# One order of products for a whole decoder trunk, with its moving averages moved to another stage

## The chip, the core and the metric

The kernel runs on one core of a Trainium2 chip. The metric is the time of one execution on the device in microseconds (us), smaller is better. Engines are named as the profile names them: PE (TensorE, the matrix engine; PEld are its weight loads), DVE (VectorE), ACT (ScalarE), POOL (GpSimd) and SP (SyncE, which only issues DMAs here).

## The reference, cut

One layer, 2048 rows of width 1024, all in 32-bit floats:

```python
mod = silu(c) @ w_ada + b_ada;  shift, scale, gate = split(mod, 3)
u = x * (1 + scale) + shift
q, k, v, a_gate, p_in, p_gate, m_a, m_p = split(u @ w_in, ...)
a = sliding_window_sink_attention(q, k, v) * silu(a_gate)      # 16 heads, window 128
a = a @ w_attn_proj
p = grouped_linear(causal_moving_average(p_in) - p_in)         # windows 2, 4, 8, 16 by group
p = (p * pool_scale) * silu(p_gate);  p = p @ w_pool_proj
y = (sigmoid(m_a) * a + sigmoid(m_p) * p) @ w_out * (1 + gate)
x = layer_norm(2 ** 0.25 * x + y)
```

The grouped linear map is folded into the pooling weights ahead of the moving average (`wmix_d`), so the average is taken of a product's result (`px_d`).

## The kernel before

**Products.** Every large matrix product is cut into blocks (`Quad`, "block" below): two weight tiles against one chunk of 1024 rows, as a 2x2 by 2x2 block product that needs seven multiplications in place of eight. A block's seven products are B11, T1 (stage F), T2, B21 (stage S), T3, B22 (stage Th) and T4 (stage L). A product is 12 matmuls of 128x512: 32-bit weights are split into a high and a low part (`w_set`: ACT casts the high part, DVE or POOL subtracts it for the low part) and three partial products are summed, four times over the depth. The seven right-hand sides are the sums of one chunk's input, held in SBUF as `set_B..`, `set_T..`. For its weight sums a block needs POOL: `sum1` (1 addition, after the load of `W` and `A22`), `mid` (2) before the split of S, `late` (1) before the split of Th. At most four `w_set` tiles live at once.

**Stages.** There are 74 blocks, 518 products. The stages are named after their tile pools: `g0` (modulation of x, keys, values; two groups of two blocks), `o0` (13 single blocks, with the attention of the first chunk laid between their matmuls: the "overlay"), `e0` (four groups of two blocks, mostly gates), the same for the second chunk (`g1`, `o1`, `e1`), then `mix`: four phases of two groups (projections) and the output phase of four groups with the layer norm. Between phases all seven sets are exchanged (`turn_sets`: each half is loaded by SP, cast by ACT, subtracted by DVE).

**What sets the order.** In `o0` and `o1` the order on each engine is the order of writing (`Ordered`, by `solos`): a block's splits stand two products ahead of their use, the first split of the next block one to two. In all stages of pairs (`ring`, `front`, `back`) a split is written directly ahead of its product, through plain `nc.scalar`, `nc.vector`, and a scheduler of the framework sets the order on ACT and DVE; `W` is loaded behind the T3 product of a block two blocks earlier. Work around the products hangs on product counts (`hooks`, `defer`). SP's queue is always in written order.

**The overlay.** After each third of a product (`beat`) a credit grows; when it reaches one, one attention step is written into PE's stream (scores, transposes, values; `lg<-kk,qs`, `pt<-ident,L`, `pv<-pth,vv`), with its softmax on DVE and ACT. Here also stand the moving averages (`window_jobs`): 32 jobs in each overlay, each of 256 columns. A job loads `vb` from `px_d`, adds 1 to 4 shifted copies on POOL (`nxt`), subtracts on DVE and stores `pw_d`. They start 25 products into the overlay. `pool_job`, in `e0` and `e1`, loads `pw_d` and the gate, multiplies, forms sums and stores them for `mix`.

```python
def window():                               # window_jobs, POOL, 256 columns
    cur, k = job["v"], 1
    while k < w:
        nx = ph.t.tile([P, 16 + C2], F32, tag="nxt", bufs=2, name="nxt")
        pool.tensor_tensor(nx[:, lo_t:], cur[:, lo_t:], cur[:, lo_t - k : 16 + C2 - k], ALU.add)
```

**Other places.** The sums of the second chunk's input (`sums_to(ph, u1_d, ...)`) are made in `e0`. The gate row of the modulation is summed in `g0` (8 loads of 512 KB, 8 reductions on DVE) and turned around through DRAM on ACT's DMA queue at the start of `g1` (`gate_rows`). In `back`, the second block of the first group of a stage begins with one extra matmul into its bank (`ph.fresh`) directly ahead of ACT's copy and of T2.

Of the kernel before, what the change touches and what calls it, by code (L numbers as in the profile page):

```python
# [19 lines left out]
P = 128  # L20
D = 1024
# [38 lines left out]
def kernel(  # L60
# [40 lines left out]
    carry = cp.tile([P, 3, 16], F32, name="carry")  # L101
# [51 lines left out]
    on = {"act": nc.scalar, "dve": nc.vector}  # L153

    def pin(flag):
        on.update({"act": act, "dve": dve} if flag else {"act": nc.scalar, "dve": nc.vector})

    class Pools:
# [33 lines left out]

        def own(self, name="x", dt=F32, tag="x"):
            return self.t.tile([P, CH], dt, tag=tag, bufs=self.bufs[tag], name=name)

        def c(self, name="c", dt=F32):
            self.n += 1
            if "more" in self.bufs and self.n % (4 + self.bufs["more"]) >= 4:
                return self.own(name, dt, "more")
            return wp.tile([P, CH], dt, tag="c", bufs=4, name=name)  # L200
# [42 lines left out]

    class Quad:
        def __init__(self, srcs, consume):
            self.srcs, self.consume = srcs, consume

        def load_w(self, ph, q=nc.sync, a12=True):
# [7 lines left out]
        def load_last(self, ph, own, q=nc.sync):  # L256
            self.a22 = ph.last(own)
            q.dma_start(self.a22, self.srcs[1][:, CH:])

        def load(self, ph, own, q=nc.sync, a12=True):  # L260
            self.w, self.a22 = ph.weights(), ph.last(own)
            x = self.w
            q.dma_start(x[:, 2, :], self.srcs[1][:, 0:CH])
            q.dma_start(self.a22, self.srcs[1][:, CH:])
            if a12:
                q.dma_start(x[:, 0::3, :], by_two(self.srcs[0]))
            else:
                q.dma_start(x[:, 0, :], self.srcs[0][:, 0:CH])

        def sum1(self, e=nc.gpsimd):  # L270
            e.tensor_tensor(self.w[:, 1, :], self.w[:, 2, :], self.a22, ALU.add)  # L271

        def mid(self, e=nc.gpsimd):
# [4 lines left out]
        def late(self, e=nc.gpsimd):  # L278
# [18 lines left out]
    def pair_split(ph, raw, a=nc.scalar, d=nc.vector):  # L297
        hi, lo = ph.split(), ph.split()
        a.copy(by_two(hi), raw)  # L299
        low(d, by_two(lo), raw, by_two(hi))  # L300
        return halves(hi, lo)

    def half_split(ph, raw, a=nc.scalar, d=nc.vector):
        s = ph.split()
        hi, lo = s[:, 0:CH], s[:, CH:]
        a.copy(hi, raw)
        low(d, lo, raw, hi)
        return hi, lo
# [19 lines left out]
    def front(ph, q, tick, beat=None):  # L328
        w = pair_split(ph, q.first())
        q.mid()  # L330
        a, b = bank(), bank()
        product(a, w[0], "B11", True, beat=beat)
        tick()
        product(b, w[1], "T1", True, beat=beat)
        tick()
        return a, b, None, None

    def back(ph, grp, opened, nxt, own, tick):
        st = []
        for x, (q, (a, b, c, w, *copy)) in enumerate(zip(grp, opened)):  # L340
            p5 = ph.p("p5")
            if w is None:
                c = bank("c1" if x else "lg")
                if x and ph.fresh:
                    t = sets["B11"][:, 0, 0, :]
                    mm(c, t[:, 0:P], t, start=True, stop=True, skip_group_check=True)
                    ph.fresh = False
                nc.scalar.copy(c, a)  # L348
                nc.scalar.copy(p5, b)
                w = pair_split(ph, q.second())[::-1]  # L350
                q.late()
                product(c, w[1], "T2")
            else:
                nc.vector.tensor_tensor(c, c, copy[0], ALU.add)
                nc.scalar.copy(p5, b)
            tick()
            nc.vector.tensor_tensor(b, c, p5, ALU.add)
            if not copy:
                product(a, w[0], "B21")
            tick()  # L360
            q.consume(ph, 0, 0, a)
            st.append((q, b, c, p5))
        w = {}

        def ask(q):
            defer(1, lambda: q.load(ph, own))
            defer(3, q.sum1)

        def third(x):
            w[x] = pair_split(ph, st[x][0].third())[::-1]  # L370
            if x < len(nxt):
                ask(nxt[x])

        def with_t3(x):
            q, b, c, p5 = st[x]
            product(c, w[x][1], "T3")
            tick()
            nc.vector.tensor_tensor(p5, c, p5, ALU.add)
            q.consume(ph, 1, 1, p5)

        def with_b22(x):
            q, b, c, p5 = st[x]
            product(b, w[x][0], "B22")
            tick()
            q.consume(ph, 0, 1, b)

        for x in range(len(st)):
            third(x)
            with_t3(x)
            with_b22(x)  # L390
        for q, b, c, p5 in st:
            w = half_split(ph, q.a22)
            product(c, w, "T4")
            tick()
            q.consume(ph, 1, 0, c)

    now, due = [0], []

    def defer(ticks, f):
        due.append((now[0] + ticks, len(due), f))  # L400

    def run_due(every=False):
        while due and (every or any(d[0] <= now[0] for d in due)):
            d = min(due, key=lambda d: d[:2])
            due.remove(d)
            d[2]()

    def ring(ph, groups, opened, hooks, nxt, after):

        pos = [0, 0]  # L410

        def tick():
            for f in hooks.get((pos[0], pos[1]), ()):
                f()
            for f in hooks.get((pos[0] - len(groups), pos[1]), ()):
                f()
            pos[1] += 1
            now[0] += 1
            run_due()

        for gi, grp in enumerate(groups):
            pos[:] = [gi, 0]
            own = gi % 2 == 0 and gi + 1 < len(groups)
            back(ph, grp, opened, (groups + [nxt])[gi + 1], own, tick)
            if gi + 1 < len(groups):
                opened = [front(ph, q, tick) for q in groups[gi + 1]]
        if after:
            return [front(ph, q, tick) for q in nxt]
        return None

    def solos(ph, quads, nxt, beat, hooks):

        seq = quads + nxt

        at = [0]

        def tick():
            for f in hooks.get(at[0], ()):
                f()
            at[0] += 1  # L440
            now[0] += 1
            run_due()

        w = pair_split(ph, seq[0].first())
        seq[0].mid()
        for i, q in enumerate(quads):
            hi, lo = ph.split(), ph.split()
            act.copy(by_two(hi), q.second())
            low(dve, by_two(lo), q.second(), by_two(hi))
            q.late(pool)  # L450
            ws = halves(hi, lo)[::-1]
            a, b = bank(), bank()
            product(a, w[0], "B11", True, beat=beat)
            c = bank()
            act.copy(c, a)
            tick()
            product(b, w[1], "T1", True, beat=beat)
            p5 = ph.p("p5")
            act.copy(p5, b)
            tick()  # L460
            hi, lo = ph.split(), ph.split()
            act.copy(by_two(hi), q.third())
            low(pool, by_two(lo), q.third(), by_two(hi))
            wt = halves(hi, lo)[::-1]
            product(c, ws[1], "T2", beat=beat)
            dve.tensor_tensor(b, c, p5, ALU.add)
            tick()
            product(a, ws[0], "B21", beat=beat)
            q.consume(ph, 0, 0, a)
            tick()  # L470
            wl = half_split(ph, q.a22, act, dve)
            product(c, wt[1], "T3", beat=beat)
            dve.tensor_tensor(p5, c, p5, ALU.add)
            q.consume(ph, 1, 1, p5)
            if i + 2 < len(seq):
                z = seq[i + 2]
                defer(1, lambda z=z: z.load_w(ph, sp))
                defer(2, lambda z=z: z.load_last(ph, False, sp))
                defer(5, lambda z=z: z.sum1(pool))
            tick()  # L480
            more = i + 1 < len(quads)
            if more:
                hi, lo = ph.split(), ph.split()
                act.copy(by_two(hi), seq[i + 1].first())
# [964 lines left out]
```

## Time and profile before

| | before |
|---|---|
| three runs | 1907.67, 1910.65, 1914.93 us (median 1910.65) |
| the profiled execution | 1913.9 us, of which its instructions span 1912.1 us |
| PE busy in it | 1723.5 us (90%), granted clock 0.959 on average |
| DVE, ACT, POOL busy | 1308.2, 932.5, 854.1 us |
| DMA | 382.19 MB, 200 GB/s |

The stages in the span: head 0 to 66.2 (eight products), rest of `g0` to 169.7, `o0` with four products of `e0` to 588.8, `e0` with four products of `g1` to 759.8, `g1` to 839.9, `o1` with four of `e1` to 1267.9, `e1` with four of `mix` to 1428.8, `mix` without and then with its output phase to 1737.8 and 1912.1. A row of a timeline gives start, length, engine, line, operation and in brackets the idle time before it and what ended it. In rows of helper functions the line is L56 (`Ordered`), so tiles name the work.

### The profile page before, as it was taken

Reading aid. Unit: us, or ns where it says so; the run is one execution under the profiler, and the core shown is the slowest. Engines: PE = TensorE matmul, PEld = TensorE weight load, DVE = VectorE, ACT = ScalarE, POOL = GpSimd, SP = SyncE. Lnnn points to the kernel's source line nnn. Section 1 sums busy time; section 2 is a strip of 40 time slices with the busy share of each in tenths; the row PEclk is TensorE's granted clock in tenths of the full one; section 3 lists DMA queues with packets and bytes.
Section 4 is the critical chain, followed back from the end, with each engine's and each line's share of the span. In section 5 each row is a group of like instructions: output and inputs, shape, how many; then the busy total and the mean of one; then the engine's idle time right before and its main releaser. Section 6 shows DMA issues by size and latency. Waiting matters only on the chain.

```text
span 1912.1 us, 25151 instructions
## 1 busy us (share of the span) xinstructions
PE 1723.5 (90%) x8061; PEld 1419.6 (74%) x8061; DVE 1308.2 (68%) x2221; ACT 932.5 (49%) x1764; POOL 854.1 (45%) x818
## 2 busy tenths in 40 slices
PE   6789999888888998799998888879999999998996
PEld 6578887676676777678887766768877777787885
DVE  5754778577663658558796776635675967769777
ACT  3444776556553335337775555523353442534452
POOL 3123354545555443453455456632232564356442
PEclk9899999999898999899999999889999999999998
DMA  8587455655346789694457544435895685767432
GB/s 320 171 266 232 133 165 181 184 155 156 118 140 221 258 304 334 222 291 158 146 175 209 165 147 133 128 105 163 292 357 165 222 274 176 242 218 264 172 133 99
DMA packets 237796, 382.19 MB, mean 200 GB/s; under 512 B 31184, under 2 KB 89312, under 8 KB 237664
## 3 DMA queue, kind: packets, MB, share of 16 engines
q1 hardware_dynamic: 233120, 371.87, 59.1%
q10 hardware_dynamic: 3232, 4.49, 0.8%
q0 software_dynamic: 1312, 4.22, 0.6%
q8 instruction: 64, 1.05, 0.2%
q14 instruction: 68, 0.56, 0.1%
HBM read 244.15 MB, written 139.49 MB: 201 GB/s over the span
## 4 chain that ended last, share of the span: by engine, by line
PE 52%; DMA 15%; DVE 13%; issue 6%; ACT 6%; POOL 5%; SPq 3%; POOLq 0%; DVEq 0%; ACTq 0%
PE mm L56 33%; PE lg L56 9%; PE c L56 7%; DMA pw_d<-nxt 3%; SPq L56 3%; PE pv L56 2%; PE pt L56 2%; DVE w_set L56 2%; DVE w_set L136 2%; ACT L L56 1%; DVE nxt L56 1%; POOL st L56 1%; DVE L L56 1%; POOL nxt L56 1%; DVE st L56 1%
## 5 line engine op out<-in xcount | busy, mean ns | idle before, releaser
L56 PE MATMUL mm<-set_B,w_set 128*128 128x512 f32 x2664 | 679.5, 401 | 48.7 <-ACT w_set L299 27.3
L56 PEld LDWEIGHTS mm<-set_B,w_set 128*128 128x128 f32 x2664 | 507.0, 193 | 166.0 <-ACT w_set L299 29.2
L56 PE MATMUL mm<-set_T,w_set 128*128 128x512 f32 x1824 | 475.6, 406 | 44.7 <-POOL w_set L56 24.4
L56 PEld LDWEIGHTS mm<-set_T,w_set 128*128 128x128 f32 x1824 | 349.4, 196 | 129.0 <-POOL w_set L56 28.3
L136 DVE TENSOR_TENSOR w_set<-W,w_set 128x1024 fp32r<-128x1024 f32 x142 | 199.5, 1407 | 155.5 <-ACT w_set L299 152.3
L299 ACT CAST w_set<-W 128x1024 fp32r<-128x1024 f32 x142 | 148.8, 1049 | 304.5 <-PE mm L56 234.9
L56 PE MATMUL c<-set_T,w_set 128*128 128x512 f32 x864 | 213.6, 396 | 22.9 <-ACT c L348 17.5
L56 PE MATMUL lg<-set_T,w_set 128*128 128x512 f32 x864 | 213.5, 395 | 4.8 <-DVE w_set L136 2.7
L56 PEld LDWEIGHTS c<-set_T,w_set 128*128 128x128 f32 x864 | 163.5, 190 | 62.0 <-ACT c L348 19.7
L56 PEld LDWEIGHTS lg<-set_T,w_set 128*128 128x128 f32 x864 | 163.3, 190 | 42.4 <-DVE w_set L136 3.5
L271 POOL TENSOR_TENSOR W<-W,A 128x512 f32<-128x512 f32 x46 | 68.6, 1492 | 269.4 <-DMA A<-in_win_dram 79.7
L56 POOL TENSOR_TENSOR W<-W 128x512 f32<-128x512 f32 x74 | 96.7, 1320 | 149.3 <-DVE w_set L56 78.1
L56 ACT ACTIVATE L<-L,nm 128x257 f32<-128x257 f32 (+1 forms) x256 | 126.8, 498 | 47.0 <-DVE nm L56 33.3
L56 ACT ACTIVATE L<-L,sm 128x256 f32<-128x256 f32 (+1 forms) x128 | 64.3, 503 | 150.8 <-DVE sm L56 150.3
L56 DVE CUSTOM_DVE_ANT_0 L<-lg,bt,nsink 128x256 f32<-128x256 f32 (+1 forms) x256 | 110.9, 469 | 38.8 <-PE lg L56 27.9
L280 POOL TENSOR_TENSOR W<-W 128x512 f32<-128x512 f32 x46 | 73.1, 1588 | 121.0 <-DVE w_set L136 113.4
L275 POOL TENSOR_TENSOR W<-W 128x512 f32<-128x512 f32 x48 | 77.5, 1615 | 107.5 <-DVE w_set L136 96.5
L56 PEld LDWEIGHTS lg<-kk,qs 128*128 128x128 f32 x512 | 80.1, 198 | 56.7 <-DVE nm L56 31.0
L56 PE MATMUL lg<-kk,qs 128*128 128x256 f32 (+1 forms) x512 | 87.4, 295 | 37.0 <-DVE nm L56 22.8
L56 DVE TENSOR_SCALAR L<-L,sm 128x256 f32<-128x256 f32 (+1 forms) x128 | 111.1, 868 | 4.5
L56 DVE TENSOR_TENSOR ptl<-pt,pth 128x512 fp32r<-128x512 f32 (+1 forms) x128 | 85.8, 670 | 31.3 <-ACT pth L56 31.0
L56 POOL TENSOR_TENSOR nxt<-nxt 128x256 f32<-128x256 f32 (+3 forms) x96 | 62.3, 649 | 82.3 <-DMA pw_d<-nxt 69.2
(216 smaller groups left out, 2583.6 us busy)
## 6 DMA issues: line engine op xcount, KB each, us to landing
W<-in_win_dram SPq DMA_DIRECT2D x40, 512.0 KB, 6.1
qs<-q_d SPq DMA_DIRECT2D x128, 128.0 KB, 3.9
W<-in_win_dram SPq DMA_DIRECT2D x46, 256.0 KB, 4.8
A<-in_win_dram SPq DMA_DIRECT2D x42, 256.0 KB, 5.0
ag_d<-sig SPq DMA_DIRECT2D x32, 256.0 KB, 3.4
q_d<-q_hi SPq DMA_DIRECT2D x32, 256.0 KB, 3.5
q_d<-q_lo SPq DMA_DIRECT2D x32, 256.0 KB, 3.9
mp_d<-sig SPq DMA_DIRECT2D x32, 256.0 KB, 6.2
```

Of the source, the lines that this page charges most:

```text
L56: return lambda *args, **kw: self.tc.keep_in_program_order(op(*args, **kw))
L136: engine.tensor_tensor(dst, src, as32(hi), ALU.subtract)
L271: e.tensor_tensor(self.w[:, 1, :], self.w[:, 2, :], self.a22, ALU.add)
L275: e.tensor_tensor(x[:, 1, :], x[:, 1, :], x[:, 0, :], ALU.subtract)
L280: e.tensor_tensor(x[:, 3, :], x[:, 3, :], x[:, 1, :], ALU.subtract)
L299: a.copy(by_two(hi), raw)
```

## The change

All phases go through one plan. `plan` lists the 518 products of all stages in order, `run` writes them out one by one on ordered queues. Each stage of a block is split two products ahead of its first product (later only where a `w_set` tile is not free); loads are tied to the block two ahead, also across phases. `ring`, `front`, `back` and `solos` go away.

- `window_jobs` and the tensor `pw_d` go away. `pool_job` now loads 512 columns of `px_d`, adds on POOL, subtracts on DVE, multiplies by the gate: 16 jobs in each of `e0` and `e1`, one every three products.
- The pooling gates pg0 and pg2 move ahead (to `g` and to the overlay), two blocks of merge gates move from there to `e`.
- The second chunk's input sums move from `e0` into `o0`, as eight `sums_job` of 256 columns.
- The gate row's sums move from `g0` to `e0`; its turn through DRAM goes from ACT's queue to SP's, the store in `e0`, the load in `g1`.
- Attention steps start after 12 beats (10 before) and come every 4.7 beats (5.2 before). Four products of the following stage no longer carry beats.
- `ph.fresh`'s extra matmul stands two stages earlier, with the copies of `c` and `p5` directly behind B11 and T1; gates of `mix` are loaded three products ahead; key tiles get room of their own.

```diff
+        for q, kind, p, k in stages:
+            mine = [slots[(n + j) % 4] for j in range(1 if kind == "L" else 2)]
+            hi = max(p - 2, mine[0] + 1, prev, 0)
+            lo = max(hi, mine[-1] + 1)
...
+        for q, z in zip(order, order[2:]):
+            p = q.at["Th"] + 1
+            loads.setdefault(p, []).append((z, "w"))
+            wait = not z.own and not q.own and not q.pair
+            limit = split_at[z] - 1
+            loads.setdefault(min(p + 1 if wait else p, limit - 1), []).append((z, "last"))
+            loads.setdefault(min(p + 4 if wait else p + 2, limit), []).append((z, "sum"))
...
-        start = [[kv_quad(s), ag[0]], [q[0], mp[0]]]
-        alone = [q[2], ag[2], x[0], x[2], q[4], ag[4], x[4], q[6], ag[6], x[6], ma[0], ma[2], ma[4]]
-        end = [[pg[0], pg[2]], [pg[4], pg[6]], [ma[6], mp[2]], [mp[4], mp[6]]]
+        start = [[kv_quad(s), ag[0]], [q[0], pg[0]]]
+        alone = [q[2], ag[2], x[0], x[2], q[4], ag[4], x[4], q[6], ag[6], x[6], pg[2], ma[0], ma[2]]
+        end = [[pg[4], pg[6]], [ma[4], ma[6]], [mp[0], mp[2]], [mp[4], mp[6]]]
...
-        rate = (N + 3) / (n_slots - 32.0)
+        rate = (N + 3) / (n_slots - 48.0)
...
+        def moving():
+            cur, k = job["v"], 1
+            while k < w:
+                nx = ph.t.tile([P, 16 + CH], F32, tag="nxt", bufs=3, name="nxt")
+                pool.tensor_tensor(nx[:, lo_t:], cur[:, lo_t:], cur[:, lo_t - k : 16 + CH - k], ALU.add)
+                cur, k = nx, 2 * k
...
+        return (0, fetch), (1, fetch_gate), (2, moving), (4, gated), (5, sums), (6, stores)
...
+            for n in range(2 * KT):
+                steps(base, 3 * n - 2, pool_job(ph, s, n // 2, n % 2, kept))
```

POOL in the middle of `o1`, before: between the block's own sums (`W`), the low part of Th (`w_set`) and the attention's sums (`st`) stand the shifted additions `nxt`.

```order
L56 TENSOR_TENSOR nxt<-vb 128x258
L56 TENSOR_TENSOR nxt<-nxt 128x256
L56 TENSOR_TENSOR st<-st,ag 128x512
L56 COPY L<-nsink 128x2
L56 TENSOR_TENSOR W<-W,A_10195 128x512
L56 TENSOR_TENSOR w_set<-W,w_set 128x1024
L56 COPY L<-nsink 128x2
L56 TENSOR_TENSOR nxt<-vb 128x262
L56 TENSOR_TENSOR nxt<-nxt 128x260
L56 TENSOR_TENSOR nxt<-nxt 128x256
```

POOL in the middle of `o1`, after:

```order
L56 TENSOR_TENSOR W<-W 128x512
L56 COPY L<-nsink 128x2
L56 TENSOR_TENSOR st<-st,ag 128x512
L56 TENSOR_TENSOR w_set<-W,w_set 128x1024
L56 TENSOR_TENSOR W<-W,A_10852 128x512
L56 COPY L<-nsink 128x2 x4
L56 TENSOR_TENSOR st<-st,ag 128x512
L56 TENSOR_TENSOR st<-st 128x512
```

The additions are gone from there, and the low part `w_set` stands ahead of the next `sum1` (`W<-W,A`), which stood ahead of it. POOL at the end of `e1`, after, where the windows are 16 wide:

```order
L56 TENSOR_TENSOR W<-W,A_12552 128x512
L56 TENSOR_TENSOR W<-W 128x512 x2
L56 TENSOR_TENSOR nxt<-vb 128x526
L56 TENSOR_TENSOR nxt<-nxt 128x524
L56 TENSOR_TENSOR nxt<-nxt 128x520
L56 TENSOR_TENSOR nxt<-nxt 128x512
L56 TENSOR_TENSOR W<-W,A_12604 128x512
L56 TENSOR_TENSOR W<-W 128x512 x2
L56 TENSOR_TENSOR nxt<-vb 128x526
```

Four additions of 512 columns now stand between the `mid` of the group's first block and the `sum1` of its second. ACT at the start of `g1`, before: `gate_d` and `cb` are DMAs on ACT's own queue, with the casts of the second block, of keys (`k_hi`) and the copy of `c` behind them.

```order
L349 COPY p_7146<-mm 128x512
L56 DMA gate_d<-mod 128x8x1
L299 CAST w_set<-W 128x1024
L56 DMA cb<-gate_d 128x1024
L538 CAST k_hi<-mm 128x512
L348 COPY c_7147<-mm 128x512
```

After, both stand in SP's queue, 33 rows apart, the first between stores of gates in `e0`:

```order
L56 DMA pg<-pg_d 128x512
L56 DMA gate_d<-mod 128x8x1
L56 DMA mp_d<-sig 128x512
L56 DMA pin_B_108<-st 128x512
L56 DMA vb<-px_d 128x512
```

ACT waits for neither any more.

More of the change, by code (lines that the diff above doesn't have):

```diff
@@ L326, in product @@
                 beat()
[L328 to L395, printed above, removed]
@@ L405, in run_due @@
             due.remove(d)
             d[2]()
[L408 to L429, printed above, removed]
@@ L497, in steps, with at @@
[L497 to L506 removed]
+    def at(p, f):
+        assert p >= now[0], (p, now[0])
+        hooks.setdefault(int(p), []).append(f)
@@ L1365 @@
[L1365 to L1382 removed]
+            steps(base, 4 + 3.3 * i, todo)
```

677 lines of the change are left out of this document (371 added, 306 removed).

## The prediction

> **What bounds the kernel now.** I read the engines' table first (PE busy 90% of the span), then the stages one by one, then PE's waits in the stages that lose most, then the chain behind such a wait. In these rows of stretches of the span the columns are: stretch, length; busy time (instructions) of PE, PEld, DVE, ACT, POOL; PE's granted clock, the DMA share and GB/s.
>
> ```profile
> 66.20:169.70 103.50, 87.69 (x441) 73.24 (x442) 59.38 (x72) 43.56 (x66) 28.19 (x29) 0.92 0.77 254
> 169.70:588.80 419.10, 370.20 (x1878) 308.91 (x1877) 287.39 (x699) 244.39 (x583) 212.50 (x259) 0.95 0.51 160
> 588.80:759.80 171.00, 159.52 (x674) 127.82 (x673) 109.36 (x107) 74.50 (x99) 74.20 (x48) 0.98 0.84 294
> 839.90:1267.90 428.00, 377.82 (x1909) 315.90 (x1908) 290.19 (x700) 250.15 (x586) 212.48 (x245) 0.94 0.52 160
> 1267.90:1428.80 160.90, 154.83 (x675) 126.04 (x674) 101.62 (x108) 66.17 (x93) 44.85 (x32) 1.00 0.74 251
> 186.00:255.00 69.00, 67.49 (x368) 57.53 (x367) 54.57 (x143) 51.21 (x123) 27.75 (x31) 1.00 0.48 150
> 925.00:1000.00 75.00, 73.17 (x404) 62.23 (x403) 62.36 (x151) 52.13 (x125) 38.80 (x43) 1.00 0.51 161
> 374.50:378.30 3.80, 0.80 (x4) 0.33 (x2) 3.59 (x3) 1.35 (x3) 3.80 (x3) 0.91 0.21 68
> 378.40:382.00 3.60, 3.59 (x9) 2.82 (x10) 3.24 (x11) 2.20 (x6) 1.38 (x3) 0.50 0.53 151
> ```
>
> PE stands idle 48.9 us in `o0` and 50.2 in `o1`, half of all its idle time (1912.1 − 1723.5 = 188.6), at clocks of 0.95 and 0.94. In `e1` it is busy 96% at full clock: there little is to be had. The sixth and seventh rows lie in the first 25 to 30 products of the overlays, where attention runs but no moving average does: PE idles 2.2 and 2.4%, the clock is full, though DVE is as busy (79 and 83%) as anywhere. So attention by itself doesn't hold PE up. The last two rows show the second loss: PE idles 3.0 of 3.8 us, and in the next 3.6 us its clock is 0.50. A mean clock of 0.95 means half clock for a tenth of the time: about 21 us lost in `o0` and 26 in `o1`, times PE's busy share of 0.88, 41 us.
>
> PE's waits in `o0` (first five rows), in `o1` (four), and two of the whole span; total, times, longest:
>
> ```profile
> PE mm L56 <- POOL w_set L56: 13.8, 5, 3.4
> PE lg L56 <- DVE nm L56: 11.4, 8, 2.7
> PE mm L56 <- ACT w_set L299: 8.8, 1, 8.8
> PE mm L56 <- ACT mm L56: 8.2, 4, 5.7
> ...
> PE mm L56 <- POOL w_set L56: 10.5, 4, 3.6
> PE mm L56 <- ACT mm L56: 7.8, 3, 5.4
> PE lg L56 <- DMA qs<-q_d: 4.5, 1, 4.5
> ...
> PE mm L56 <- DVE w_set L136: 20.8, 11, 4.2
> PE c L56 <- ACT c L348: 17.5, 5, 11.2
> ```
>
> The wait of 8.8 for ACT stands in `o1` too, once each, at the overlay's entry, where the first split isn't yet two ahead. What is behind a wait for POOL's `w_set`, by the chain of waits (start, length, row, idle before):
>
> ```profile
> 442.25 1.31 POOL L56 TENSOR_TENSOR nxt<-nxt 128x260 f32<-128x260 f32 x2 [3.93 <-DMA pw_d<-nxt]
> 443.52 1.27 POOL L56 TENSOR_TENSOR W<-W,A 128x512 f32<-128x512 f32 x1
> 444.75 2.52 POOL L56 TENSOR_TENSOR w_set<-W,w_set 128x1024 fp32r<-128x1024 f32 x1
> 447.33 1.88 PE L56 MATMUL mm<-set_T,w_set 128*128 128x512 f32 x7 [3.27 <-POOL w_set L56]
> ```
>
> POOL stood 3.93 us at a moving average that waited for the store of an earlier one (`pw_d`, whose buffer it needs); the block's own sum and the low part queued behind it, and PE waited 3.27. The same by the tile `nxt`:
>
> ```profile
> L56 POOL TENSOR_TENSOR nxt<-nxt x96: 612/626/1003, 338.2 to 1239.4; 128x256 f32<-128x256 f32 x48, 128x260 f32<-128x260 f32 x16, 128x268 f32<-128x268 f32 x16, 128x264 f32<-128x264 f32 x16
> L56 POOL TENSOR_TENSOR nxt<-vb x64: 603/621/1333, 273.5 to 1237.3; 128x256 f32<-128x256 f32 x16, 128x258 f32<-128x258 f32 x16, 128x262 f32<-128x262 f32 x16, 128x270 f32<-128x270 f32 x16
> L56 DVE SCALAR_TENSOR_TENSOR nxt<-nxt,vb x64: 415/426/1582, 274.4 to 1240.2; 128x256 f32<-128x256 f32 x64
> ...
>   DMA pw_d<-nxt: 69.2, 29
> ...
>   DMA vb<-px_d: 39.6, 22
> ```
>
> POOL works 96 × 0.626 + 64 × 0.621 = 100 us on them and idles 69 + 40 at transfers of theirs, all in the overlays.
>
> **The change, part by part.**
>
> **Window jobs out of the overlays.** Ceiling: all matmuls of the overlays at the quiet stretches' rate. 368/69.0 = 5.33 and 404/75.0 = 5.39 per us, mean 5.36. The two rows have 1878 + 1909 − 96 (eight products of the pair stages at their ends) = 3691; at 5.36 that is 689 us. Now they take 419.1 + 428.0 − 22 (the 96, at `e1`'s 154.83/675 = 0.229 us) = 825. Ceiling: −136. Beside it: idle 99 less the 16 that stay (2.3% of 689), plus 41 of half clock, is 124. Floor: only the waits that name the causes removed, POOL's `w_set` 13.8 + 10.5 and the entries 2 × 8.8, 42 us, with their share of the half clock (41 × 42/99 = 17): −59. I take −104, nearer to the ceiling, because waits that name others (`lg<-DVE nm`, `mm<-ACT mm`) come from engines which stand in order behind a late `w_set` too, and in the quiet stretches they are about 1 us each. Short of the ceiling, because attention is now denser (a step in 4.7 beats, not 5.2: a tenth more DVE work per us, and DVE stood at 83% in the seventh row), and the entry and the last blocks aren't quiet stretches. The rule for Th (`w_set` ahead of the next `sum1`) brings another 1.27 us earlier on this chain and is in that sum.
>
> The Trainium skill, "TensorE: Matmul & The Clock Gate", Part 1, section "What's actually happening", says that the clock halves after an idle window of about 3.4 us and comes back after as long a busy one. By that alone only the longest waits above would cost half clock, seven at most, 1.7 us each: 12, not 41, and the time would come out near 1800. The row at 378.40 shows 0.50 behind 3.0 us of idleness, and the mean clocks ask for 41: the measurement decides.
>
> **The gate row off ACT's queue.** In `g1`, before:
>
> ```profile
> 764.52 0.40 ACTq L56 DMA_DIRECT2D gate_d<-mod  x1
> 775.81 0.59 ACT L538 CAST k_hi<-mm 128x512 fp32r<-128x512 f32 x1 [9.36 <-DMA gate_d<-mod]
> 776.94 4.63 PE L56 MATMUL c<-set_T,w_set 128*128 128x512 f32 x12 [11.16 <-ACT c L348]
> ```
>
> The load of `cb` waits in ACT's queue for the store, with the cast and `c` behind it: PE stands 11.16 us. On SP's queue the store lies in `e0`, the load a stage later. −11, plus some half clock (4.63 us for twelve matmuls is 0.39 each, not 0.23), not counted. What it could cost: SP's queue waits for the store's source while loads of gates stand behind it, some 10 us; they are issued three products ahead (8.3 us) now. Bounds −13 to 0.
>
> **`g0`.** Its 8 loads of 512 KB and 8 reductions leave. The stage's dearest wait was PE's 6.70 us for an ACT cast:
>
> ```profile
> 99.73 5.46 PE L56 MATMUL mm<-set_B,w_set 128*128 128x512 f32 x12 [6.70 <-ACT w_set L299]
> ```
>
> −5 of it (bounds −7 to 0: the first loads stay). In `e0` the reductions are hidden: DVE is busy 109 of 171 us there. The loads add 4 MB to a stage of 50, from which the sums' traffic leaves.
>
> **`fresh` and the copies earlier.** Of the 17.5 us in `c<-ACT c`, 11.2 are counted; −6 (0 to −6).
>
> **Pair stages split two products ahead.** PE waits 20.8 us there for DVE's low part (`L136`), in 11 waits. A cast and a low part cost, by group:
>
> ```profile
> L299 ACT CAST w_set<-W 128x1024 fp32r<-128x1024 f32 x142 | 148.8, 1049 | 304.5 <-PE mm L56 234.9
> L136 DVE TENSOR_TENSOR w_set<-W,w_set 128x1024 fp32r<-128x1024 f32 x142 | 199.5, 1407 | 155.5 <-ACT w_set L299 152.3
> ```
>
> 1.05 + 1.41 = 2.46 us, inside two products (24 × 0.229 = 5.5). I take half, −10 (bounds −20 to +10), since the splits now run in a fixed order and need their sums earlier: what is late next is the load of `W`.
>
> **Windows inside `e0` and `e1`.** Groups of four jobs with 1, 2, 3 and 4 additions: 40 additions of 512 columns a stage. The nearest row is a sum of that shape:
>
> ```profile
> L271 POOL TENSOR_TENSOR W<-W,A x46: 1287/1302/2277, 75.0 to 1848.3; 128x512 f32<-128x512 f32 x46
> ```
>
> 40 × 1.302 = 52 us on a POOL that is busy 74 of 171 us (less with the sums gone) and 45 of 161: room on the mean. In the last twelve products a job has 4 × 1.3 = 5.2 us in three products (8.3 us), and the blocks' own four additions in seven products take 2.2 of every 8.3: 90%. A `sum1` or `gated` behind a job comes late there: +4 a stage, +8 (bounds 0 to +58, below). DVE's part (16 subtractions of 512 columns, by the row of `nxt` on DVE 2 × 0.426 each, 14 us on 102 of 161) is hidden.
>
> **The sums in `o0`.** Eight jobs, some 20 us of POOL, where POOL is busy 213 of 419 us and loses half of the 100 + 109 above. Hidden, unless the loads bunch.
>
> Sum: −104 − 11 − 5 − 6 − 10 + 8 = −128. The profiled execution spans 1912.1 us and took 1913.9; the median of runs is 1910.65, 0.2% below. I take the 128 from that: 1783.
>
> **The rivals.**
>
> (a) POOL at its slow rate in `e0`, `e1`. The same addition takes 1.27 us mostly, but where DVE works beside it 2.28:
>
> ```profile
> 579.35 1.27 POOL L276 TENSOR_TENSOR W<-W 128x512 f32<-128x512 f32 x1
> ...
> 755.36 2.28 POOL L280 TENSOR_TENSOR W<-W 128x512 f32<-128x512 f32 x1
> ```
>
> Then a job of four takes 9.1, the sums 3.9 in 8.3 us: 4.7 short, four times; a job of three 2.4 short, four times: 29 a stage, 58, against the 8 taken: 1783 + 50 = 1833. For it: the end of `e0` is where that row stands. Against it: `L271`'s mean, 1.302, with a worst of 2.277. The Trainium skill, "GPSIMD Engine Reference", § 8 "Key points", has POOL share its SBUF interfaces with DVE and contend with DVE instructions of two inputs; the two rows agree with that.
>
> (b) Attention binds. The steps are denser, and `lg<-DVE nm` (11.4 in each overlay) is their own chain. Then the overlays give the floor only: 1783 + 45 = 1828. Against it: 0.6 us or so of that wait in the quiet stretches.
>
> (c) Slower. Two products ahead, a pair stage has about three products (8.3 us) from a load's issue to the split's end:
>
> ```profile
> W<-in_win_dram SPq DMA_DIRECT2D x40, 512.0 KB, 6.1
> ```
>
> 6.1 + 1.3 + 1.05 + 1.41 = 9.9, with POOL's slow sum 10.8: 2.5 late; with the load stretched by 0.6 (DMA share 0.84 in `e0`) the wait passes 3.0 and draws 3.4 us of half clock after it: 6.5. In 24 pair groups, once each, +156: 1939. It decides above 128/24 = 5.3 us a group. Against it: loads are issued a block and more ahead where buffers are free, and the overlay, whose splits stand two ahead already, has no wait of such a kind in its quiet stretches.
>
> (d) The change doesn't do what it says: `w_set` tiles aren't free earlier (four live) and splits begin where they did (0, not −10), the denser attention takes what the additions give in the overlays (0, not −104) and the sums in `e` what `g1` gives (+11): −128 + 125 = −3, about 1908. Against it stand the quiet stretches; hardly.
>
> **How the numbers follow.** The forecast 0.60, (a) 0.13, (b) 0.17, (c) 0.05, (d) 0.03, and 0.02 for the ceiling in all terms. The forecast's own range: overlays at −136 (1751) to −70 (1817). 8 in 10 are held by 1748 to 1850, which takes in (a) and (b). 0.5% (9.6 us) is about what can be told from no change: faster 0.92, same 0.03 (d), slower 0.05 (c).
>
> **What the profile after would show.** Right: `o0` and `o1` at PE 95% or more and a clock of 0.98, no `nxt` on POOL there, waits for POOL's `w_set` under 5 us in each; `g1` without its 11 us; `e0`, `e1` within 10 us of 171 and 161. Wrong: in `e0`/`e1` sums (`W`) at 2.28 us and PE waiting for POOL or for ACT's cast behind it (a); `lg<-DVE nm` above 11 us in the overlays with DVE over 85% (b); waits of 2 to 4 us for `w_set` once a group in `g`, `e`, `mix`, with `W`'s load as what ended them (c).

## The result, and the profile after

The changed kernel takes 1878.96 us (median of four runs, 1876.99 to 1880.95) against 1909.18 for the kernel before (median of four too, one run more than in the table above): a ratio of 0.984, 95% interval 0.981 to 0.986. It is faster by 30 us, where 128 were forecast; 1879 lies outside the range of 1748 to 1850. The profiled execution spans 1875.2 us, 36.9 less than before.

The same stages in the profile after (head, `g0`, `o0`, `e0`, `g1`, `o1`, `e1`, `mix`, output phase; columns as before):

```profile
0.00:67.10 67.10, 49.49 (x224) 40.66 (x224) 45.24 (x109) 30.52 (x49) 14.10 (x40) 0.95 0.60 228
67.10:185.20 118.10, 94.79 (x441) 77.53 (x442) 48.59 (x60) 43.32 (x67) 15.86 (x13) 0.87 0.59 185
185.20:549.40 364.20, 343.69 (x1830) 290.31 (x1829) 262.57 (x670) 252.89 (x596) 175.20 (x191) 0.99 0.59 185
549.40:727.30 177.90, 161.52 (x674) 128.41 (x672) 132.15 (x127) 59.93 (x86) 112.31 (x87) 0.97 0.75 234
727.30:821.20 93.90, 83.52 (x346) 66.52 (x346) 63.85 (x57) 37.39 (x52) 49.87 (x33) 0.95 0.79 266
821.20:1181.40 360.20, 345.73 (x1862) 294.85 (x1861) 264.30 (x671) 245.92 (x578) 155.95 (x163) 0.99 0.51 162
1181.40:1352.20 170.80, 158.52 (x674) 127.85 (x673) 117.83 (x110) 60.69 (x86) 102.89 (x72) 0.98 0.69 215
1352.20:1671.10 318.90, 310.17 (x1346) 252.29 (x1345) 227.79 (x213) 128.86 (x153) 149.80 (x94) 0.99 0.67 226
1671.10:1875.20 204.10, 164.66 (x673) 130.42 (x671) 138.84 (x177) 73.71 (x108) 79.63 (x50) 0.91 0.37 134
```

An overlay now ends four products earlier; they stand in `g1` and `mix` instead (and in `e0`, `e1` four are exchanged for four). Four products are 48 matmuls of 0.229 us, 11.0 us. With this the stages compare so:

| stage | before, us | after, us | difference |
|---|---|---|---|
| head, `g0` | 66.2, 103.5 | 67.1, 118.1 | +0.9, +14.6 |
| `o0` + `o1` | 847.1 − 22.0 = 825.1 | 724.4 | −100.7 |
| `e0`, `e1` | 171.0, 160.9 | 177.9, 170.8 | +6.9, +9.9 |
| `g1` | 80.1 + 11.0 = 91.1 | 93.9 | +2.8 |
| `mix` | 309.0 + 11.0 = 320.0 | 318.9 | −1.1 |
| output phase | 174.3 | 204.1 | +29.8 |

The overlays did what was forecast, at PE 94 and 96% and a clock of 0.99. The stages of pairs, which should have given 24 us, cost 63, nearly half of it in the output phase, for which the sum had no term of its own. PE's waits after, in `g0` (two rows), `o0`, `g1` and the output phase (two):

```profile
PE pt L56 <- ACT vt L56: 7.1, 1, 7.1
PE pv L56 <- ACT st L56: 4.4, 3, 3.0
...
PE mm L56 <- POOL w_set L56: 0.9, 1, 0.9
...
PE pt L56 <- ACT vt L56: 4.8, 1, 4.8
...
PE mm L56 <- ACT w_set L56: 15.2, 4, 4.1
PE lg L56 <- DVE w_set L56: 3.5, 3, 1.6
```

POOL's `w_set` no longer holds PE in `o0`, and the waits of 8.8 us at the overlays' entries are gone. New are ACT's `vt` in `g0` and `g1`, and ACT's casts in the output phase, which had 4.2 us of waits in all before.

### The profile page after: what moved, and what is told of

Read it like the earlier page. It is cut to its first block, busy times and chain, and to the rows that moved or that the text cites. A ratio compares the mean times of both kernels' runs of the same rounds, so it can differ in the third digit from the quotient of the medians.

```text
span 1875.2 us, 24894 instructions
## 1 busy us (share of the span) xinstructions
PE 1712.1 (91%) x8061; PEld 1408.8 (75%) x8061; DVE 1301.2 (69%) x2191; ACT 933.2 (50%) x1773; POOL 855.6 (46%) x738
## 5 line engine op out<-in xcount | busy, mean ns | idle before, releaser
L56 PE MATMUL mm<-set_B,w_set 128*128 128x512 f32 x2664 | 685.6, 403 | 46.0 <-ACT w_set L56 28.3
L56 PEld LDWEIGHTS mm<-set_B,w_set 128*128 128x128 f32 x2664 | 508.5, 194 | 169.2 <-ACT w_set L56 33.3
L56 POOL TENSOR_TENSOR W<-W 128x512 f32<-128x512 f32 x216 | 317.8, 1486 | 431.2 <-DVE w_set L56 293.8
L56 PE MATMUL mm<-set_T,w_set 128*128 128x512 f32 x1824 | 458.4, 395 | 18.9 <-ACT mm L56 15.6
L56 PEld LDWEIGHTS mm<-set_T,w_set 128*128 128x128 f32 x1824 | 339.3, 190 | 93.8 <-ACT mm L56 19.4
L56 DVE TENSOR_TENSOR w_set<-W,w_set 128x1024 fp32r<-128x1024 f32 x196 | 274.3, 1399 | 171.6 <-ACT w_set L56 157.2
L56 ACT CAST w_set<-W 128x1024 fp32r<-128x1024 f32 x222 | 232.2, 1046 | 225.8 <-POOL W L56 136.5
L56 PE MATMUL lg<-set_T,w_set 128*128 128x512 f32 x864 | 216.0, 396 | 17.6 <-DVE w_set L56 14.0
L56 PE MATMUL c<-set_T,w_set 128*128 128x512 f32 x864 | 215.2, 396 | 13.2 <-DVE w_set L56 12.1
L56 PEld LDWEIGHTS lg<-set_T,w_set 128*128 128x128 f32 x864 | 163.1, 191 | 58.4 <-DVE w_set L56 19.5
L56 POOL TENSOR_TENSOR W<-W,A 128x512 f32<-128x512 f32 x72 | 103.9, 1443 | 220.0 <-DMA A<-in_win_dram 135.7
L56 PEld LDWEIGHTS c<-set_T,w_set 128*128 128x128 f32 x864 | 163.2, 191 | 53.1 <-DVE w_set L56 17.3
L56 ACT ACTIVATE L<-L,nm 128x257 f32<-128x257 f32 (+1 forms) x256 | 126.8, 498 | 25.8 <-DVE nm L56 25.8
L56 DVE CUSTOM_DVE_ANT_0 L<-lg,bt,nsink 128x256 f32<-128x256 f32 (+1 forms) x256 | 110.8, 469 | 20.9 <-PE lg L56 15.8
L56 DVE TENSOR_SCALAR L<-L,sm 128x256 f32<-128x256 f32 (+1 forms) x128 | 110.0, 860 | 4.5
L56 ACT ACTIVATE L<-L,sm 128x256 f32<-128x256 f32 (+1 forms) x128 | 64.4, 503 | 94.9 <-DVE sm L56 94.9
L56 DVE TENSOR_TENSOR ptl<-pt,pth 128x512 fp32r<-128x512 f32 (+1 forms) x128 | 85.7, 670 | 28.1 <-ACT pth L56 26.8
L56 ACT ACTIVATE sig<-mm 128x512 f32<-128x512 f32 x76 | 45.4, 598 | 109.9 <-PE mm L56 108.3
L56 PEld LDWEIGHTS lg<-kk,qs 128*128 128x128 f32 x512 | 78.3, 192 | 27.2 <-DVE nm L56 13.9
L56 DVE TENSOR_TENSOR w_set<-A,w_set 128x512 fp32r<-128x512 f32 x74 | 63.2, 854 | 47.0 <-ACT w_set L56 47.0
L56 PE MATMUL lg<-kk,qs 128*128 128x256 f32 (+1 forms) x512 | 83.5, 286 | 11.7 <-DVE nm L56 8.8
L56 ACT CAST pth<-pt 128x512 fp32r<-128x512 f32 (+1 forms) x128 | 72.4, 565 | 30.9 <-PE pv L56 30.2
```

What stands on the lines that cost most here:

```text
L56: return lambda *args, **kw: self.tc.keep_in_program_order(op(*args, **kw))
```

## The experiments

Stages that an edit doesn't touch show how far one profile can be read: with the same instructions `e0` took 177 to 183 us, `g1` 89 to 95, `mix` 319 to 325, the output phase 204 to 207. A difference under some 5 us in one stage of one run tells nothing.

**Did the windows cost the overlays?** The kernel before, with the jobs of `window_jobs` never written and `px_d` loaded (the moving averages are left out):

```diff
-            sp.dma_start(x, cols(pw_d[m], 2 * s + t))
+            sp.dma_start(x, cols(px_d[m], 2 * s + t))
...
-                    for at, f in part:
-                        hooks.setdefault(25 + 8 * m + 2 * c + at, []).append(f)
+                    pass
```

> The kernel before without its window jobs in the overlays (the moving averages are left out: the pool jobs load px_d directly). Theory A (the windows on POOL, with their trip through DRAM, cost the overlays what the change got back): o0 and o1 go from 419 and 428 us to about 375 each, so -90 to -105 us, about 1810. Rival B (the overlays gained by the other parts, the earlier low part of Th, the start with both splits ahead, denser attention): at most half of it, -50 us or less.

1830.72 us; `o0` and `o1` in its profile, and the waits that remain in `o0`:

```profile
168.70:543.90 375.20, 354.47 (x1877) 300.08 (x1876) 258.62 (x667) 244.01 (x582) 156.41 (x163) 0.98 0.50 156
797.10:1185.30 388.20, 362.26 (x1910) 306.69 (x1909) 262.12 (x668) 250.55 (x587) 159.16 (x165) 0.97 0.49 154
```

```profile
PE mm L56 <- ACT w_set L299: 8.8, 1, 8.8
PE mm L56 <- POOL w_set L56: 4.5, 2, 3.4
```

847.1 − 763.4 = 84 us of the 101 are the windows alone (additions, subtractions and their DMAs): nearer to theory A than to B, though below A's 90 to 105. The entry's wait of 8.8 us stands in each overlay here and in none after; two of them are as much as the other 17, but that they are its cause was not tried by itself, nor was the denser attention.

**The output phase.** First, the splits of the next product written ahead of the side work of the same tick (a tick is one product's place in the order; `splits(p)` writes what `before[p]` holds):

```diff
                 behind(ph, q, kind, h)
+            if p + 1 not in starts:
+                splits(p + 1)
             tick()
```

> The changed kernel with one edit: the splits that stand ahead of a product are written before the side work of the same tick (hooks and deferred jobs: layer norm steps, gate sums, pool jobs), not behind it. Nothing is left out. Theory A (in ordered queues a split stands behind side work that waits): the three waits of 4.1 us for ACT's cast at the second block of the output groups shrink to under 1 us each, and with the half clock behind them the output phase goes from 204 us to about 182; e0 and e1 lose a few us each; in all -20 to -35 us against the changed kernel's 1879, so about 1850. Rival B (the splits are late because their sums or loads are late, POOL or DMA): no change within 5 us, the waits stay and name POOL's sums.

1911.29 us, ratio to before 1.000 (0.998 to 1.001): 32 us slower than the changed kernel. Theory A fell, and so did B's "no change". Most of the loss lies in `e0` (192 us) and `e1` (179), 21 us together, where PE's waits for ACT's casts rose from 3.9 to 17.8 us and from 3.1 to 13.2; the output phase went to 208. PE's waits there:

```profile
PE mm L56 <- ACT w_set L56: 10.9, 5, 3.7
PE lg L56 <- ACT w_set L56: 8.7, 3, 3.2
```

The waits at the first split became shorter (2.1 us each where they were 4.1), but others of 2.7 to 3.2 us appeared at the next split: a cast that is written early itself waits for POOL's sum (ACT's casts stood 13.4 us at such sums in this phase, 7.4 in the changed kernel), and now the norm waits behind the cast. What the chain is, the timeline of the changed kernel shows (DVE, POOL, ACT, then PE's wait):

```profile
1720.85 1.92 DVE L56 SCALAR_TENSOR_TENSOR wide<-wide,mean,wide 128x1024 f32<-128x1024 f32 x1
1722.70 0.14 DVE L56 TENSOR_SCALAR mean<-total 128x1 f32<-128x1 f32 x1
1722.76 0.14 DVE L56 TENSOR_SCALAR down<-total 128x1 f32<-128x1 f32 x1
...
1720.40 1.29 POOL L56 TENSOR_TENSOR W<-W,A 128x512 f32<-128x512 f32 x1
...
1723.01 1.15 ACT L56 ACTIVATE spare<-wide,down 128x1024 f32<-128x1024 f32 x1 [1.23 <-DVE down L56]
1724.07 0.19 ACT L56 ACTIVATION_READ_ACCUMULATOR spare<-wide,down 128x1 f32 x1
1724.16 1.04 ACT L56 ACTIVATE wide<-wide 128x1024 f32<-128x1024 f32 x1
1725.10 0.19 ACT L56 ACTIVATION_READ_ACCUMULATOR wide<-wide 128x1 f32 x1
1725.20 1.03 ACT L56 CAST w_set<-W 128x1024 fp32r<-128x1024 f32 x1
...
1726.28 0.73 PE L56 MATMUL mm<-set_B,w_set 128*128 128x512 f32 x2 [4.11 <-ACT w_set L56]
```

ACT's squares (`spare`) wait for `down`, a step of 0.14 us that stands in DVE's queue behind a row's scaling of 1.92 us. The next row's sums (`wide`) and the cast stand behind the squares in ACT's queue: the cast begins at 1725.20, though POOL's last sum ahead of it had ended at 1721.69, and PE waits 4.11 us. The norm's steps were kept in written order before too (L56), but the casts, low parts and block sums (L299, L136, L275) were not. The squares' wait in this phase, before and after:

```profile
L56 ACT ACTIVATE spare<-wide,down 128x1024 f32<-128x1024 f32 x13 | 15.0, 1154 | 21.6 <-DVE down L56 21.6
...
L56 ACT ACTIVATE spare<-wide,down 128x1024 f32<-128x1024 f32 x13 | 15.0, 1151 | 38.6 <-DVE down L56 38.6
```

Second, then, the norm's steps taken apart, one engine to a step and a product between (the small tiles also get six buffers in place of two, as a row now takes longer):

```diff
-        def squares():
+        def means():
             dve.tensor_scalar(mean, total, 1.0 / D, None, ALU.mult)
             dve.tensor_scalar(down, total, -1.0 / D, None, ALU.mult)
+        def squares():
             act.activation(ph.spare(), z, AF.Square, bias=down, accum_out=rs)
...
-        for at, f in ((1, sums), (2, squares), (3, power), (4, scale), (6, store)):
+        for at, f in ((1, sums), (2, means), (3, squares), (4, variance), (5, power), (6, scale), (8, store)):
```

> The changed kernel with the layer norm's steps taken apart: each step's instructions stand on one engine and one product behind those that feed them (sums on ACT, means on DVE, squares on ACT, variance on DVE, power on POOL, both scalings on DVE), so that no engine's queue waits for another within a step. Nothing is left out. Theory C (in ordered queues ACT, DVE and POOL wait for each other in the norm's chain, and casts and sums of the next group stand behind it): the three waits of 4.1 us go, the output phase falls from 204 us to about 180, so about 1856. Rival D (POOL's and DVE's own work in this phase, sums at 1.9 us, is what is too slow): under 6 us.

1858.87 us, ratio to before 0.973 (0.968 to 0.978); the output phase, its stretch and PE's waits for ACT there:

```profile
1667.00:1851.80 184.80, 157.97 (x673) 126.03 (x672) 135.43 (x177) 73.92 (x108) 72.28 (x50) 0.96 0.42 148
```

```profile
PE mm L56 <- ACT w_set L56: 2.8, 1, 2.8
```

Theory C: 19 of the 30 us come back with the same instructions on each engine, PE's waits for ACT's casts fall from 15.2 to 2.8 us and the clock rises from 0.91 to 0.96. (The six buffers were not tried by themselves.) Of the other 10 us PE's waits make 7 (11.1 us against 4.2 before, 8.0 of them for DVE, 0.5 to 1.5 each); why they are there stays open.

**`e0` and `e1`.** Without the shifted additions:

```diff
-            cur, k = job["v"], 1
+            cur, k = job["v"], w
```

> The changed kernel without the shifted additions on POOL in e0 and e1 (the moving averages are left out; loads, subtractions, gates and stores stay). Theory A (POOL's windows make DVE and their own sums slow in the e stages): e0 goes from 178 to about 168 and e1 from 171 to about 161, their time before, together -17 to -20 us; DVE's w_set there falls from up to 2.06 us to 1.2. Rival B (only the new fixed order with DVE's gates and splits in it): under 5 us for both.

1842.9 us; `e0`, `e1`:

```profile
549.80:708.30 158.50, 154.58 (x674) 125.68 (x674) 114.60 (x128) 60.36 (x86) 52.79 (x47) 1.00 0.85 260
1160.50:1316.50 156.00, 154.18 (x675) 126.91 (x675) 105.66 (x110) 60.65 (x86) 47.76 (x32) 0.99 0.74 234
```

348.7 − 314.5 = 34 us, nearly twice what theory A expected: without additions both stages are faster than before, PE at 98 and 99%. So the rest of the change gave 17 us in them (331.9 − 314.5; the second chunk's sums, which left `e0`, are part of it), and the additions took 34. Is it the bunch of four in one product? One addition a product, the gate step two products later:

```diff
-        return (0, fetch), (1, fetch_gate), (2, moving), (4, gated), (5, sums), (6, stores)
+        return (
+            (0, fetch), (2, lambda: moving(1)), (3, lambda: moving(2)), (4, lambda: moving(4)), (5, lambda: moving(8)),
+            (4, fetch_gate), (6, gated), (7, sums), (8, stores),
+        )
```

> The changed kernel with the shifted additions of a pool job in e0 and e1 written one a product in place of all in one product (gate two products later). Same work. Theory E (a block's sums stand behind up to four additions, 6 us, on POOL): e0 goes from 178 to about 165 and e1 from 171 to about 160, two thirds of the 34 us that leaving the additions out gave; about 1856. Rival F (it is POOL's and DVE's amount of work beside each other, not the queue): under 8 us for both.

1880.23 us, ratio 0.984 (0.980 to 0.988), as the changed kernel; `e0` 177.3, `e1` 166.8 us. Theory E fell, rival F (under 8 us) held. Is it DVE, standing in order at a gate step that waits for POOL? The gate step reading the loaded columns (the averages are made and not used):

```diff
-            job["s"] = cur
+            job["s"] = job["v"]
```

> The changed kernel in which the gate step of a pool job reads the loaded columns in place of POOL's result (the averages' result is left unused; all additions still run on POOL). Theory K (DVE stands in order at a gate step that waits for POOL, with splits behind it): e0 and e1 lose most of the 34 us that leaving the additions out gave, 20 or more. Rival L (it is POOL's own work: the blocks' sums come late behind and beside the additions, and DVE only passes it on): under 10 us together.

1867.4 us, `e0` + `e1` 174.8 + 163.8 = 338.6: −10, at theory L's edge, though DVE's waits for POOL's additions in the two stages fell from 21.1 to 2.6 us. And half of the columns added (the other half of the averages is left out), DVE still waiting, 9.6 us:

```diff
-                pool.tensor_tensor(nx[:, lo_t:], cur[:, lo_t:], cur[:, lo_t - k : 16 + CH - k], ALU.add)
+                pool.tensor_tensor(nx[:, lo_t : 16 + CH // 2], cur[:, lo_t : 16 + CH // 2], ..., ALU.add)
...
```

> The changed kernel with the shifted additions on half of the columns only (256 of 512; the other half of the averages is left out, the gate step takes it from the loaded columns in an instruction of its own, so DVE still waits for POOL). Theory L (the amount of POOL's work sets the loss): e0 + e1 give back half or more of the 34 us, 17 to 28. Theory K (DVE's standing at POOL does): under 10.

1857.65 us, 167.8 + 157.9 = 325.7: −23, two thirds of the 34 for half of the work. As almost all of DVE's waits for POOL are worth 10 at most, this is theory L in the main, the amount of POOL's work. By the groups of the changed kernel and of the one without additions (`e0`):

```profile
L56 POOL TENSOR_TENSOR nxt<-nxt 128x512 f32<-128x512 f32 (+3 forms) x24 | 35.0, 1460 | 1.9
L56 DVE TENSOR_TENSOR w_set<-W,w_set 128x1024 fp32r<-128x1024 f32 x23 | 37.6, 1636 | 24.6 <-ACT w_set L56 24.5
```

```profile
L56 DVE TENSOR_TENSOR w_set<-W,w_set 128x1024 fp32r<-128x1024 f32 x24 | 32.1, 1338 | 24.7 <-ACT w_set L56 24.6
```

An addition took 1.46 us, not 1.30, and DVE's low part 1.64 us beside them, 1.34 without; in `e1` (after, and without additions):

```profile
L56 DVE TENSOR_TENSOR w_set<-W,w_set 128x1024 fp32r<-128x1024 f32 x24 | 36.9, 1538 | 25.8 <-ACT w_set L56 22.2 <-DMA pin_B<-st 3.5
```

```profile
L56 DVE TENSOR_TENSOR w_set<-W,w_set 128x1024 fp32r<-128x1024 f32 x24 | 31.5, 1314 | 32.3 <-ACT w_set L56 31.9 <-DMA A<-in_win_dram 0.4
```

It is the low part that PE mostly waits for in `e`: 11.8 of 15.7 us in `e0`, where it waits 2.0 in all without additions. The two largest rows, after:

```profile
PE lg L56 <- DVE w_set L56: 5.1, 3, 2.4
PE c L56 <- DVE w_set L56: 4.1, 4, 2.3
```

Single rows of `e0` show what the mean hides, a low part beside POOL's additions and one while POOL stands idle:

```profile
641.72 3.89 POOL L56 TENSOR_TENSOR nxt<-nxt 128x516 f32<-128x516 f32 x2
642.66 2.05 DVE L56 TENSOR_TENSOR w_set<-W,w_set 128x1024 fp32r<-128x1024 f32 x1
...
682.54 1.26 POOL L56 TENSOR_TENSOR W<-W,A 128x512 f32<-128x512 f32 x1
684.92 1.23 DVE L56 TENSOR_TENSOR w_set<-W,w_set 128x1024 fp32r<-128x1024 f32 x1 [6.26 <-ACT w_set L56]
686.22 1.66 POOL L56 TENSOR_TENSOR W<-W 128x512 f32<-128x512 f32 x1 [2.42 <-DVE w_set L56]
```

Of the 23 low parts there, nine had none of POOL's work beside them and took 1.22 us; the other 14 took 1.90 on average. How much of the 34 is slower instructions and how much late sums was not taken apart.

**Two products ahead, in the stages of pairs.**

```diff
-            hi = max(p - 2, mine[0] + 1, prev, 0)
+            hi = max(p - (1 if q.pair else 2), mine[0] + 1, prev, 0)
```

> The changed kernel with the splits of the pair stages one product ahead in place of two; the single blocks of the overlays stay at two. Nothing is left out. Theory M (the second product of lead was worth the 10 us forecast, most of it in the stages with little side work): the mix stage goes from 319 to about 324 and the whole is 8 to 15 us slower. Rival N (in a fixed order the lead is worth more than forecast, since what stands ahead of a split waits too): 30 us or more slower. Rival O (it is worth nothing: tiles and sums set when a split can run): within 5 us.

1946.19 us, ratio to before 1.019 (1.016 to 1.022): 67 us slower than the changed kernel, +17 in `mix`, +16 each in `e0`, `e1` and the output phase. Rival N. `mix` takes the same time with a lead of two as it did before, with splits directly ahead of their products in the scheduler's order; so in a fixed order the second product of lead seems to make up only for what that order did. That is read from one stage, and no run shows it by itself.

**`g1` and `g0`.** The gate row's DMAs back on ACT's queue:

```diff
-            sp.dma_start(cb, gate_d.rearrange("k p -> (k p)").partition_broadcast(P))
+            act.dma_start(gate_d.rearrange("k p -> p k"), mod[:, 16:24], ...)
+            act.dma_start(cb, gate_d.rearrange("k p -> (k p)").partition_broadcast(P))
...
```

> The changed kernel with the gate row's store and load back on ACT's queue at the start of g1. Theory I (the move was worth the 11 us forecast, and the wait for the store of values in g1 is another matter): g1 goes from 94 to about 105. Rival J (ACT would stand at the one or the other, and the move is worth less because splits two ahead cover it): under 5 us more.

1887.69 us, `g1` 99.6, +5.7 on 93.9: between I and J, about half of the 11, and at the edge of what one profile can tell. The second tile of values in another ring (a set of buffers used in turn), so that it doesn't take `v_hi`'s buffer:

```diff
-                vt = ph.c("vt")
+                vt = ph.c("vt") if t else ph.p("vt")
```

> The changed kernel with one edit: the second tile of values (vt of the half 0) takes a buffer of the ring p in place of one of the ring c, whose earlier user is v_hi, so that ACT no longer waits for the store of v_hi. Nothing is left out. Theory A (moving the keys to a buffer of their own shifted the ring c, and ACT now stands at a store of 7 us): PE's waits of 7.1 us in g0 and 4.8 us in g1 for ACT's vt go, with the half clock behind them g0 loses 9 to 11 us (118 to about 108) and g1 6 to 8 (94 to about 87). Rival B (the store's slow landing only shows there; the next thing that takes a buffer of the ring waits for the same stores): under 3 us in g0 and g1 together.

1874.29 us. `vt`'s waits are gone in both, but `g1` gained only 3.0 us (90.9) and `g0` 1.7 (116.4), no more than these stages differ between runs: in `g0` PE's waits for the next cast, of `room_k`, rose from 3.0 to 8.1 us. Theory A fell; rival B fits `g0`. The stores of the folded weights and the bias loads back on their queues of before:

```diff
-                sp.dma_start(dst, st)
+                pool.dma_start(dst, st)
...
-            at(base + 10 + j, lambda j=j: spread_bias(j))
+            at(base + 7 + j // 4, lambda j=j: spread_bias(j))
```

> The changed kernel with the stores of the folded pooling weights back on POOL's queue, and the loads of the spread bias back on ACT's queue in two bunches ahead of the folds, as before. Theory G (g0 lost 15 us because these stores wait in SP's queue and the loads stand between ACT's copies): g0 goes from 118 to about 106. Rival H (the folds' copies and casts stand in a fixed order on ACT behind evictions that wait for PE): g0 above 113.

1872.37 us, `g0` 114.9, by its number rival H; PE's waits for ACT's `st` and `room_k` fell, `vt`'s rose from 7.1 to 10.6. Then three edits together (norm, `vt`, queues):

> The changed kernel with three of the edits tried: the norm's steps taken apart, the second tile of values in the ring p, and g0's stores and bias loads on their queues of before. Nothing is left out. If the causes add, -19 in the output phase, -4 to -10 in g0 and -3 in g1: 1846 to 1853, faster than both kernels. If what g0 waits for only changes its name again, -20 in all, about 1859.

1854.28 us, ratio 0.971 (0.968 to 0.973), just above the 1846 to 1853 expected if the causes add, as `g0` took 117.3, with one wait of 12.9 us: ACT's queue issued the bunched bias loads for 12.0 us and then stood at the store of `v_hi`. The `vt` edit and the folded weights' stores on POOL's queue alone, without the bunch:

> The changed kernel with the second tile of values in the ring p and the stores of the folded pooling weights on POOL's queue; the bias loads stay one a product. Nothing is left out. Theory G2 (two waits for stores, of v_hi and of the folded weights, cost g0 its 15 us; the bunch of bias loads was what spoilt the run with three repairs): g0 goes from 118 to about 108. Rival H (each of these waits has another behind it, so their sum doesn't come back): g0 above 113.

```profile
68.80:175.20 106.40, 88.29 (x442) 72.40 (x443) 51.41 (x60) 42.76 (x67) 26.74 (x26) 0.94 0.67 213
```

1873.5 us, `g0` 106.4: theory G2, 12 of the 15 us. Last, the norm's steps, spread additions, `vt` and these stores together:

> The changed kernel with the norm's steps taken apart, the additions of pool jobs one a product, the second tile of values in the ring p and the folded weights' stores on POOL's queue. Nothing is left out. If they add: -19 in the output phase, -4 in e0 and e1, -3 in g1 and -3 to -10 in g0: 1843 to 1852. If the spread additions only move waits (as their own run suggested): about 1855.

1852.28 us, ratio to before 0.968 (0.964 to 0.972), at the slow end of the 1843 to 1852 expected if the parts add: faster than both kernels, though not to be told from the norm's steps alone (0.968 to 0.978). `g0` took 110.0 there at a clock of 0.88 with the same waits (19.9 us of gaps, 20.4 in the run above, where the clock was 0.94). The output phase took 187 us, `e0` 178, `e1` 169.

## Why the prediction was wrong, point by point

Of the 91 us between the forecast of −128 and the spans' −36.9, 30 lie in the output phase, 26 in the price of the additions, 20 in `g0` and 14 in `g1`.

- **Overlays, −104**: −100.7 measured, 84 of it the windows. The reading from the quiet stretches held. Rival (b) did not come: PE's waits for `nm` fell to 5.8 and 2.9 us.
- **Window additions in `e0`, `e1`, +8**: they cost 34. This is the mis-sized term. It counted only the last twelve products, where POOL's queue would be full; but the loss is by amount of work over the whole stage, and the working left out that DVE's low part gets slower beside POOL (1.34 to 1.64 us), which is what PE waits for. Its price of 1.302 us was the median of `L271`, read as the mean, which is 1.49. The bound of 58 did hold the loss. Rival (a) had the place right and the price too high (2.28 us; the mean was 1.40 to 1.47). The sign that `e0` and `e1` would stay within 10 us came true by luck: the additions' 34 stood against 17 that the rest gave.
- **Pair stages two ahead, −10, and `fresh`, −6**: 17 came in the `e` stages once the additions are taken out, not all of it from these two, and 1 in `mix`; in the output phase there was no gain. PE's waits for ACT's copies of `c`, 17.5 us before, are gone; what that gave was not tried by itself. Against a lead of one, the second product is worth 67 us in the changed kernel. The working named the fixed order, but expected of it only late loads of `W`.
- **The output phase, no term of its own**: +30. The prediction gave it only its share of the −10, though the change put the casts, low parts and block sums into the same fixed order as the layer norm's chain over three engines. This is the step that failed most: only edits were costed, not what the fixed order does to code that wasn't edited. 19 of the 30 come back when the chain is taken apart; the other 10 stay open. Rival (c) had waits in pair stages, but at loads of `W`; the chains shown here run through the side work of other queues.
- **`g0`, −5**: +14.6. What leaves was counted, not what two small moves do: the keys' own buffer shifted the ring `c`, so that `vt` takes a buffer whose store hasn't landed, and the stores of the folded weights joined SP's queue. Undone together they gave 12 in one run and 8 in another. The wait of 6.7 us that the term was taken from did go; PE's longest for a split's cast there is 2.3 after.
- **`g1`, −11**: the wait for the gate row went, and another for a store (`vt`, 4.8 us) stood behind it; undone, the edit costs about 6. Why the stage gained nothing is open: without `vt`'s wait it took 90.9, as much as before the change (91.1).
- **The sum** of the measured differences: −100.7 (overlays) + 14.6 (`g0`) + 16.8 (`e0`, `e1`) + 2.8 (`g1`) − 1.1 (`mix`) + 29.8 (output phase) + 0.9 (head) = −36.9, the difference of the two spans.

## What to carry to other kernels

Where a change replaces a scheduler's order by a written one, go through each stage's side work, edited or not: here a step in which one engine waited for another held all that was queued behind it, and writing each step on one engine, a product behind what feeds it, gave back 19 us without touching the work. Price work that moves to a shared engine by its total over the whole stage, and leave it out once to measure it; spreading it didn't help, halving it did. When a ring of buffers changes its users, ask of each tile whose store must have landed before it can be written.

## What the runs showed of the hardware

POOL's work made DVE's low part slower: in `e0` of the changed kernel it took 1.22 us with none of it beside and 1.90 on average with some, in `e1` 1.22 and 1.91. The other way round too: of the 40 additions in `e0`, ten that met nothing on DVE took 1.13 us, the others 1.58.

The clock's loss doesn't follow from the sum of the gaps: with nearly equal waits (19.9 and 20.4 us) `g0` ran at 0.88 in one run and 0.94 in another, 3.6 us apart. Nor does it need a gap of 3 us: with the splits written first, PE waited 2.13 us in the output phase, and just behind that the clock was 0.50 for 3.3 us:

```profile
1755.06 0.98 PE L56 MATMUL mm<-set_B,w_set 128*128 128x512 f32 x2 [2.13 <-ACT w_set L56]
...
1755.40:1758.70 3.30, 3.02 (x8) 1.90 (x7) 2.25 (x5) 0.96 (x1) 2.35 (x2) 0.50 0.00 0
```

The prediction's rival (c) had set 3.0 us as what draws half clock.
